# Moving the next block's norm behind attention, sending its scale through DRAM, and letting merge gates run up to six tiles ahead

## The chip, the cores and the metric

The kernel runs on one core of a Trainium2 chip. The metric is the device time of one execution in microseconds (us), as the median of several runs. Engines: PE (TensorE, matmuls), DVE (VectorE), ACT (ScalarE), POOL (GpSimd) and SP (SyncE, which here issues every DMA). Each engine works through its own instructions in order.

## The reference, cut to what matters

One layer of a hybrid decoder trunk over x of 2048 tokens by 1024 channels, in float32:

```python
h = _rmsnorm(x, norm_w[l])                    # x * rsqrt(mean(x*x) + EPS) * w
proj = h @ w_in[l]                            # three mixers' inputs and the merge gates' logits
y_a = _hgrn2_branch(...)                      # gated linear recurrence
y_b = _gated_deltanet_branch(...)             # chunked delta rule
y_c = _swa_sink_branch(...)                   # sliding-window attention
lifted = jnp.einsum('bsnc,ncd->bsnd', ys, w_branch[l])
gates = jax.nn.sigmoid(gate_logits.reshape(Bn, S, N_BRANCHES, D_MODEL))
merged = jnp.sum(gates * lifted, axis=2)
x = x + merged @ w_out[l]
...
return _rmsnorm(x, final_norm)
```

## The kernel before, in words

The 2048 tokens go through in four blocks of 512, block 0 to block 3 (`block(s, ...)`, called at the end of `_trunk`). Most operands are kept channel-major: a tile is 128 channels by 512 tokens. Every float32 product is done as three matmuls on a high and a low part (lines 101 to 103 in `mm_ct`, lines 169 to 171 in `mm_tc`), so one projection of 1024 channels onto 128 outputs is 24 matmuls of 512 columns (two weight tiles `wHL` of 12 matmuls each), and one lift of a branch's 512 channels is 12 (one weight tile). `load_w` (line 77) loads the weight tiles; there are four slots (`WB`). Block 0 loads raw weights, splits them on ACT and DVE and stores the split pair; blocks 1 to 3 load the stored pair (`wHL<-kept`, 512 KB).

A block runs, in the order in which it is written: four units of branch A, four of branch B (`unit_b`), four of branch C (`unit_c`, attention), with `merge(0)`, `merge(1)` and `merge(2)` after each branch. `merge(n, yT)` goes over eight tiles of 128 output channels. Per tile: a gate projection, which reads only the block's h (`hH`, `hL`); a tanh on ACT into `gth` (line 352; two slots); the lift of the branch's output y (lines 101 to 103 again, on `yH`, `yL`), whose 12 matmuls go by head, three for each of the four units of the branch; the product of both on DVE (line 358, and 361 from `merge(1)` on); and the sum into `msum` on POOL (line 362). A `gth` slot is free again when POOL has summed it. The gates and lifts use the PSUM tag `d`, which has four banks.

The next block's norm stands between `c0`, `c1` and `unit_c(2)`: eight tiles of x are loaded (`load_x`, line 126, two slots `xs`), ACT squares them and sums along the row (line 128), POOL adds the two halves and takes the power -1/2 (lines 132, 115, 116), POOL forms four diagonal tiles (line 137), PE multiplies them by ones (line 138), and ACT copies the result to R (line 140), which holds each token's scale in every partition. After `merge(2)`, `norm_h` multiplies the transposed x tiles by R on DVE (line 153; three `xT` slots), and splits them into `hH` and `hL` on ACT and DVE (lines 106, 107); those two are single-buffered. `output()` then multiplies the merged tiles by the output weights. Block 3 has no next block and so no norm at that place.

The order on each engine is not the written one. A list scheduler takes, on each engine, the first instruction in written order that its own model of the durations calls ready, subject to the slot counts, and that order is then fixed: an engine that waits at run time for one instruction doesn't take a later one. `tc.issue_after(i)` puts what is written inside it behind instruction i on i's engine.

Of the kernel before, what the change touches and what calls it, by code (L numbers as in the profile page):

```python
# [11 lines left out]
F32 = mybir.dt.float32  # L12
# [4 lines left out]
ALU = mybir.AluOpType  # L17
# [3 lines left out]
P = 128  # L21
D = 1024
KT = D // P
TB = 512
NT = TB // P
BW = 512
EPS = 1e-6
# [4 lines left out]
WB = 4  # L32
NTC = 324
SBK = 65
BSTEP = 16 * SBK
SLOT = ("w0", "w1", "w2", "w3", "w4", "w5", "w7", "raw")

# [14 lines left out]
def _trunk(tc, S, a, out):  # L52
    nc = tc.nc
# [4 lines left out]
    sb = _Aligned(ctx.enter_context(tc.tile_pool(name="sb", bufs=2)))  # L58
    ps = ctx.enter_context(tc.tile_pool(name="ps", bufs=4, space=PSUM))
    dram = ctx.enter_context(tc.tile_pool(name="dram", bufs=1, space=DRAM))  # L60

    V, A, G, T = nc.vector, nc.scalar, nc.gpsimd, nc.tensor
# [9 lines left out]
    def bank(tag="d", w=None):  # L72
        return ps.tile([P, 512], F32, name="ps_" + tag, tag=tag, bufs=4 if tag == "d" else 2)
# [16 lines left out]
                nc.sync.dma_start(kept[key], w[:, :, :n].bitcast(F32))  # L90
        return w[:, 0, :n], w[:, 1, :n]

    last_mm, last_act, last_ld = [None], [None], [None]

    def mm_ct(p, src, rh, rl, nk):
        for q in range(nk // 4):
# [8 lines left out]
    def split(dst_h, dst_l, src, scale):  # L105
        A.activation(dst_h, src, AF.Copy, scale=scale)
        V.scalar_tensor_tensor(dst_l, src, scale, dst_h.bitcast(F32), op0=ALU.mult, op1=ALU.subtract)
# [5 lines left out]
    def rsq(dst, src, mul, add, exp=mhalf4):  # L113
        n = src.shape[-1]
        G.tensor_scalar(dst, src, mul, add, op0=ALU.mult, op1=ALU.add)
        G.tensor_tensor(dst, dst, exp[:, :n], op=ALU.pow)
# [6 lines left out]
    def load_x(s, sq, i, tag="xs"):  # L123
        j, half = i // 2, i % 2
        t = sb.tile([P, TB], F32, name="xs", tag=tag, bufs=2)
        nc.sync.dma_start(t, a["x"][s * TB + j * P:s * TB + (j + 1) * P, half * TB:(half + 1) * TB])
        scrp = sb.tile([P, TB], BF16, name="scrp", tag="scrp", bufs=1)
        A.activation(scrp, t, AF.Square, accum_out=sq[:, j, half:half + 1])

    def norm_scale(sq):  # L130
        rs = sb.tile([P, NT], F32, name="rsx", tag="rsx")
        G.tensor_tensor(rs, sq[:, :, 0], sq[:, :, 1], op=ALU.add)
        rsq(rs, rs, 1.0 / D, EPS)
        rp = bank("c0")
        for j in range(NT):
            dg = sb.tile([P, P], F32, name="dg", tag="vn")
            G.tensor_tensor(dg, ident, rs[:, j:j + 1].broadcast_to([P, P]), op=ALU.mult)
            T.matmul(rp[:, j * P:(j + 1) * P], onesP, dg, start=True, stop=True)
        R = sb.tile([P, TB], F32, name="R", tag="R", bufs=1)
        A.copy(R, rp)  # L140
        return rs, R

    def load_xT(s, kt, tag="xT", bufs=3):
        t = sb.tile([P, TB], F32, name="xT", tag=tag, bufs=bufs)
        nc.sync.dma_start(t, a["xT"][kt, :, s * TB:(s + 1) * TB])
        return t

    def norm_h(R, xT, eng=(V, V)):
        hH = sb.tile([P, KT, TB], F32R, name="hH", tag="hH", bufs=1)
        hL = sb.tile([P, KT, TB], F32R, name="hL", tag="hL", bufs=1)  # L150
        for kt in range(KT):
            t = xT(kt)
            eng[kt % 2].tensor_tensor(t, t, R, op=ALU.mult)
            split(hH[:, kt, :], hL[:, kt, :], t, normw[:, kt:kt + 1])
        return [hH[:, kt, :] for kt in range(KT)], [hL[:, kt, :] for kt in range(KT)]
# [69 lines left out]
    gscr = dram.tile([NH, TB], F32, name="gscr", tag="gscr")  # L225
    zb = sb.tile([P, NT * SBK], F32, name="zb", tag="w2")
    G.memset(zb, 0.0)
    scrN = [dram.tile([2 * NT * NT, BSTEP], F32, name="scrN%d" % k, tag="scrN%d" % k) for k in range(2)]
    scrX = [dram.tile([2 * NT * NT, BSTEP], F32, name="scrX%d" % k, tag="scrX%d" % k) for k in range(2)]
    for t in scrX:  # L230
        flat = bass.AP(tensor=t.tensor, offset=t.offset, ap=[[NT * SBK, P], [1, NT * SBK]])
        nc.sync.dma_start(flat, zb[:, 0:NT * SBK])
    convw = cload("convw", a["convw"])
# [80 lines left out]
    def block(s, hH, hL, last=None):  # L314
# [32 lines left out]
        def merge(n, yT):  # L347
            yH, yL = [[t[:, k, :] for k in range(4)] for t in yT]
            for dt in range(KT):
                gp = proj_ct(37 + n * KT + dt)  # L350
                th = sb.tile([P, TB], F32, name="gth", tag="gth", bufs=2)
                A.activation(th, gp, AF.Tanh, scale=0.5)  # L352
                lp = bank()
                mm_ct(lp, a["wb"][n, dt], yH, yL, 4)
                if n == 0:
                    m = sb.tile([P, TB], F32, name="msum", tag="msum", bufs=KT + 1)
                    msum.append(m)
                    V.scalar_tensor_tensor(m, th, 1.0, lp, op0=ALU.add, op1=ALU.mult)
                else:
                    m = msum[dt]  # L360
                    V.scalar_tensor_tensor(th, th, 1.0, lp, op0=ALU.add, op1=ALU.mult)  # L361
                    G.tensor_tensor(m, m, th, op=ALU.add)  # L362
                if n == 2:
                    mH.append(sb.tile([P, TB], F32R, name="mH", tag=SLOT[dt]))
                    mL.append(sb.tile([P, TB], F32R, name="mL", tag="msum", bufs=KT + 1))
                    split(mH[dt], mL[dt], m, 0.5)
# [122 lines left out]
        def unit_b(h):  # L489
# [53 lines left out]
            for c2 in range(2):  # L543
# [4 lines left out]
                for ci in range(2):  # L548
# [12 lines left out]
            sN, sX = scrN[h % 2], scrX[h % 2]  # L561
            half = lambda t, r: bass.AP(tensor=t.tensor, offset=t.offset + (r // 64) * NT * 4 * BSTEP,
                                        ap=[[64, 64], [4 * BSTEP, NT], [1, 64]])
            diag = lambda t: bass.AP(tensor=t.tensor, offset=t.offset, ap=[[BSTEP, 32], [64, 16], [1, 16]])
            for r in (0, 64):
# [172 lines left out]
        def output():  # L738
            rt = [[None, None] for _ in range(NT)]
            sq = sb.tile([P, NT, 2], F32, name="sq", tag="sq")  # L740
            for half in range(2):
                fs = slice(half * 512, half * 512 + 512)
                for j in range(NT):
                    t = sb.tile([P, 512], F32, name="rt", tag=SLOT[half * 4 + j])
                    nc.sync.dma_start(t, a["x"][t0 + j * P:t0 + (j + 1) * P, fs])
                    rt[j][half] = t
                pj = mm_tc(a["wo"][half], 512, mH, mL, 4 if half and s == NSB - 1 else 1)
                for j in range(NT):
                    t = rt[j][half]
                    V.tensor_tensor(t, pj[j], t, op=ALU.add)  # L750
                    scrp = sb.tile([P, TB], BF16, name="scrp2", tag="scrp", bufs=1)
                    A.activation(scrp, t, AF.Square, accum_out=sq[:, j, half:half + 1])
                    if half == 0:
                        G.tensor_tensor(t, t, fnorm[:, fs], op=ALU.mult)
                    elif s == NSB - 1 and j < NT - 1:
                        V.tensor_tensor(t, t, fnorm[:, fs], op=ALU.mult)

            def final():
                for j in range(NT):
                    ss = sb.tile([P, 1], F32, name="ss2", tag="ss2", bufs=4)  # L760
                    G.tensor_tensor(ss, sq[:, j, 0:1], sq[:, j, 1:2], op=ALU.add)
                    rsq(ss, ss, 1.0 / D, EPS)
                    for half in range(2):
                        fs = slice(half * 512, half * 512 + 512)
                        t = rt[j][half]
                        if half == 0 or (s == NSB - 1 and j < NT - 1):
                            A.activation(t, t, AF.Copy, scale=ss)
                        else:
                            V.scalar_tensor_tensor(t, t, ss, fnorm[:, fs], op0=ALU.mult, op1=ALU.mult)
                        nc.sync.dma_start(out[t0 + j * P:t0 + (j + 1) * P, fs], t)  # L770
            return final
# [32 lines left out]
        f3(yB)  # L804
        c1 = unit_c(1)
        merge(1, yB)
        yC = new_y()
        c0(yC)
        c1(yC)
        if s + 1 < NSB:  # L810
            sq = sb.tile([P, NT, 2], F32, name="sqx", tag="sqx")
            with tc.issue_after(last_ld[0]):
                for i in range(2 * NT):
                    load_x(s + 1, sq, i)
            R = norm_scale(sq)[1]
        unit_c(2)(yC)
        unit_c(3)(yC)
        merge(2, yC)
        if s + 1 < NSB:
            return norm_h(R, lambda kt: load_xT(s + 1, kt)) + (output(),)  # L820
        output()()

    for s in range(NSB):
# [90 lines left out]
```

## Time and profile before

| | us |
|---|---|
| median of 3 runs | 2516.06 (2513.42 to 2519.41) |
| the profiled execution, device time | 2514.51 |
| its span, first to last instruction | 2512.7 |
| PE busy in the span | 2428.6 (97%) |
| DVE, ACT, POOL busy | 1170.9, 869.2, 434.2 |
| mean granted TensorE clock | 0.984 of full speed |

The span is the time between the first and the last instruction of the profiled execution; 1.8 us of the device time lie around it. A busy PE in these views is a PE with a matmul in flight: consecutive matmuls overlap and their ends are modelled, so that short waits between them hide in the busy time.

### The profile page before, as it was taken

The numbers are of one execution on the slowest core, as the hardware profiler recorded it, in microseconds if no ns is written. First come the engines' busy times: TensorE is split into PE (matmuls) and PEld (weight loads), VectorE is DVE, ScalarE is ACT, GpSimd is POOL, SyncE is SP. The second block draws the span as 40 slices with busy tenths as digits, with TensorE's granted clock in tenths as the row PEclk, the third lists the DMA queues.
The fourth block names the chain that finished last, engine by engine and source line by source line (L and its number), as shares of the span: only waits on it lengthen the run. The fifth ranks groups of instructions, "written<-read, shape, count | busy, mean of one in ns | idle before, by whom it ended". The sixth has DMA issues, their size and how long they took to land. (4 is left out here: it accounts for less than half of the span.)

```text
span 2512.7 us, 37478 instructions
## 1 busy us (share of the span) xinstructions
PE 2428.6 (97%) x13658; PEld 1946.4 (77%) x13658; DVE 1170.9 (47%) x3188; ACT 869.2 (35%) x2288; POOL 434.2 (17%) x821
## 2 busy tenths in 40 slices
PE   8999998999999999899999999989999999998998
PEld 7777776778877777678887877767888787876886
DVE  5666575465345535524214553551322455455321
ACT  5454344444334313323223422332322342233221
POOL 3221011211222101111112210111111221111111
PEclk9999998999999999999999999999999999999999
DMA  7756673769944455264774455425566354442555
GB/s 244 247 193 224 221 260 96 241 221 336 299 134 130 154 161 158 83 208 148 247 218 127 139 156 165 146 88 193 167 228 210 122 155 149 160 150 87 176 193 175
DMA packets 193156, 452.84 MB, mean 180 GB/s; under 512 B 52243, under 2 KB 70588, under 8 KB 192844
## 3 DMA queue, kind: packets, MB, share of 16 engines
q1 hardware_dynamic: 192972, 450.45, 55.3%
q8 instruction: 108, 1.77, 0.3%
q14 instruction: 76, 0.62, 0.1%
HBM read 348.81 MB, written 103.14 MB: 180 GB/s over the span
## 5 line engine op out<-in xcount | busy, mean ns | idle before, releaser
L101 PE MATMUL ps_d<-hH,wHL 128*128 128x512 f32 x1952 | 785.6, 402 | 4.1 <-DVE mm L700 2.2
L102 PE MATMUL ps_d<-hL,wHL 128*128 128x512 f32 x1952 | 783.5, 401 | 0.0
L103 PE MATMUL ps_d<-hH,wHL 128*128 128x512 f32 x1952 | 779.9, 400 | 0.7 <-DVE wHL L87 0.7
L101 PEld LDWEIGHTS ps_d<-hH,wHL 128*128 128x128 f32 x1952 | 369.4, 189 | 77.5 <-DVE mm L700 3.9
L103 PEld LDWEIGHTS ps_d<-hH,wHL 128*128 128x128 f32 x1952 | 369.3, 189 | 71.8 <-issue 1.8
L102 PEld LDWEIGHTS ps_d<-hL,wHL 128*128 128x128 f32 x1952 | 369.4, 189 | 68.0 <-issue 1.7
L87 DVE TENSOR_TENSOR wHL<-wraw,wHL 128x512 fp32r<-128x512 f32 (+1 forms) x194 | 130.6, 677 | 93.3 <-ACT wHL L86 91.2
L362 POOL TENSOR_TENSOR msum<-msum,gth 128x512 f32<-128x512 f32 x64 | 88.6, 1387 | 443.6 <-DVE gth L361 443.6
L101 PE MATMUL ps_d<-yH,wHL 128*128 128x512 f32 x384 | 155.3, 406 | 5.8 <-ACT yH L342 3.7
L86 ACT CAST wHL<-wraw 128x512 fp32r<-128x512 f32 (+1 forms) x194 | 113.7, 590 | 130.9 <-PE ps_d L103 80.8
L103 PE MATMUL ps_d<-yH,wHL 128*128 128x512 f32 x384 | 154.9, 403 | 0.0
L102 PE MATMUL ps_d<-yL,wHL 128*128 128x512 f32 x384 | 153.8, 401 | 0.1
L352 ACT ACTIVATE gth<-ps_d 128x512 f32<-128x512 f32 x96 | 57.3, 597 | 256.9 <-PE ps_d L103 256.1
L361 DVE SCALAR_TENSOR_TENSOR gth<-gth,ps_d 128x512 f32<-128x512 f32 x64 | 43.9, 687 | 184.9 <-PE ps_d L103 177.4
L169 PE MATMUL ps_d<-wHL,mH 128*128 128x512 f32 x256 | 99.7, 391 | 1.3 <-DMA wHL<-kept 1.3
L502 DVE SCALAR_TENSOR_TENSOR qkB<-raw,convw,qkB 128x512 f32<-128x512 f32 x96 | 71.7, 746 | 61.2 <-ACT qkB L500 59.9
L170 PE MATMUL ps_d<-wHL,mH 128*128 128x512 f32 x256 | 99.6, 389 | 0.0
L171 PE MATMUL ps_d<-wHL,mL 128*128 128x512 f32 x256 | 99.5, 389 | 0.0
L101 PEld LDWEIGHTS ps_d<-yH,wHL 128*128 128x128 f32 x384 | 73.0, 191 | 21.8 <-ACT yH L342 4.6
L102 PEld LDWEIGHTS ps_d<-yL,wHL 128*128 128x128 f32 x384 | 73.6, 192 | 15.9 <-DVE yL L343 1.7
L103 PEld LDWEIGHTS ps_d<-yH,wHL 128*128 128x128 f32 x384 | 73.5, 191 | 15.2 <-issue 0.5
L402 PEld LDWEIGHTS ps_c<-qk 128*64 128x64 f32 x1536 | 52.6, 137 | 33.3 <-issue 20.4
(281 smaller groups left out, 3761.0 us busy)
## 6 DMA issues: line engine op xcount, KB each, us to landing
wHL<-kept SPq DMA_DIRECT2D x486, 512.0 KB, 3.6
kept<-wHL SPq DMA_DIRECT2D x162, 512.0 KB, 4.0
wraw<-in_wct_dram SPq DMA_DIRECT2D x122, 256.0 KB, 3.7
wHL<-kept SPq DMA_DIRECT2D x32, 324.0 KB, 4.1
xT<-in_xT_dram SPq DMA_DIRECT2D x32, 256.0 KB, 4.6
xs<-in_x_dram SPq DMA_DIRECT2D x32, 256.0 KB, 4.4
rt<-in_x_dram SPq DMA_DIRECT2D x32, 256.0 KB, 4.6
out_dram<-rt SPq DMA_DIRECT2D x32, 256.0 KB, 4.0
```

The costliest lines, as they stand in the source:

```text
L86: A.copy(w[:, 0, :n], raw[:, :n])
L87: V.tensor_tensor(w[:, 1, :n], raw[:, :n], w[:, 0, :n].bitcast(F32), op=ALU.subtract)
L101: T.matmul(p, wh[:, ks], rh[kt], start=(kt == 0), stop=False)
L102: T.matmul(p, wh[:, ks], rl[kt], start=False, stop=False)
L103: last_mm[0] = T.matmul(p, wl[:, ks], rh[kt], start=False, stop=(kt == nk - 1)).ins
L169: T.matmul(pj[j][:, :n], lh[kt][:, js], wh, start=(kt == 0), stop=False)
L170: T.matmul(pj[j][:, :n], lh[kt][:, js], wl, start=False, stop=False)
L171: T.matmul(pj[j][:, :n], ll[kt][:, js], wh, start=False, stop=(kt == KT - 1))
L352: A.activation(th, gp, AF.Tanh, scale=0.5)
L362: G.tensor_tensor(m, m, th, op=ALU.add)
L402: T.matmul(sp[g * 64:g * 64 + 64, c * 32:(c + 1) * 32], K[:, c * P + g * 64:c * P + g * 64 + 64], qv[:, c, g * nb // 2:(g + 1) * nb // 2, ...
L502: V.scalar_tensor_tensor(dst, raw[:, j:j + TB], convw[:, ti, j:j + 1], dst, op0=ALU.mult, op1=ALU.add)
```

## The change

`norm_scale` is no longer called between blocks (only at the start of the kernel). The loads of x, the squares and POOL's sum and power now stand behind `unit_c(2)` and `unit_c(3)` and in front of `merge(2)`. In place of POOL's diagonal tiles, the matmuls by ones and the copy on ACT, SP writes the 512 scales to a row in DRAM (4 from each of 128 partitions) and reads that row back into all 128 partitions. `norm_h`'s DVE instructions are put behind the last line-361 instruction of `merge(2)`. The slots of `gth` go from two to six, in all three merges.

```diff
+GB = 6
...
+    rscr = dram.tile([TB], F32, name="rscr", tag="rscr")
+
+    def norm_row(sq):
+        rs = sb.tile([P, NT], F32, name="rsx", tag="rsx")
+        G.tensor_tensor(rs, sq[:, :, 0], sq[:, :, 1], op=ALU.add)
+        rsq(rs, rs, 1.0 / D, EPS)
+        nc.sync.dma_start(rscr.rearrange("(j p) -> p j", p=P), rs)
+        R = sb.tile([P, TB], F32, name="R", tag="R", bufs=1)
+        nc.sync.dma_start(R, rscr.rearrange("(o t) -> o t", o=1).broadcast_to([P, TB]))
+        return R
...
-                th = sb.tile([P, TB], F32, name="gth", tag="gth", bufs=2)
+                th = sb.tile([P, TB], F32, name="gth", tag="gth", bufs=GB)
...
-                    V.scalar_tensor_tensor(th, th, 1.0, lp, op0=ALU.add, op1=ALU.mult)
+                    last_dve[0] = V.scalar_tensor_tensor(th, th, 1.0, lp, op0=ALU.add, op1=ALU.mult).ins
...
         c1(yC)
+        unit_c(2)(yC)
+        unit_c(3)(yC)
         if s + 1 < NSB:
             sq = sb.tile([P, NT, 2], F32, name="sqx", tag="sqx")
             with tc.issue_after(last_ld[0]):
                 for i in range(2 * NT):
                     load_x(s + 1, sq, i)
-            R = norm_scale(sq)[1]
-        unit_c(2)(yC)
-        unit_c(3)(yC)
+            R = norm_row(sq)
         merge(2, yC)
         if s + 1 < NSB:
-            return norm_h(R, lambda kt: load_xT(s + 1, kt)) + (output(),)
+            with tc.issue_after(last_dve[0]):
+                hs = norm_h(R, lambda kt: load_xT(s + 1, kt))
+            return hs + (output(),)
         output()()
```

## Rows read from the trace of the kernel before

**Rows 1.** The page: span, busy times of the engines, granted clock in 40 slices.
```profile
span 2512.7 us, 37478 instructions
PE 2428.6 (97%) x13658; PEld 1946.4 (77%) x13658; DVE 1170.9 (47%) x3188; ACT 869.2 (35%) x2288; POOL 434.2 (17%) x821
...
PEclk9999998999999999999999999999999999999999
```

**Rows 2.** Busy time by window, merge 1's last line 361 to merge 2's first; blocks 0-3.
```profile
core 0: us, PE busy (x) PEld busy (x) DVE busy (x) ACT busy (x) POOL busy (x), PEclk, DMA share, GB/s
499.90:552.90 53.00, 50.94 (x279) 40.21 (x278) 32.63 (x95) 26.25 (x71) 6.25 (x12) 0.97 0.64 224
1117.30:1173.00 55.70, 51.05 (x292) 40.94 (x291) 24.94 (x82) 23.72 (x66) 5.80 (x13) 0.97 0.42 141
1736.50:1793.60 57.10, 51.66 (x292) 41.34 (x291) 24.98 (x83) 23.13 (x64) 5.78 (x13) 0.94 0.41 135
2356.30:2404.70 48.40, 48.37 (x283) 38.80 (x282) 24.07 (x79) 19.80 (x55) 1.68 (x1) 1.00 0.40 131
```

**Rows 3.** Waits of PE (who for whom: total us, times, longest us).
```profile
PE ps_c L138 <- POOL dg L137: 14.3, 5, 5.4
```

**Rows 4.** The norm of block 1 in order of time (start, us; in brackets idle before).
```profile
1124.65 0.63 ACT L128 ACTIVATE scrp<-xs 128x512 bf16<-128x512 f32 x1 [1.70 <-DMA xs<-in_x_dram]
...
1128.33 0.20 POOL L132 TENSOR_TENSOR rsx<-sqx 128x4 f32<-128x4 f32 x1 [8.98 <-ACT scrp L128]
...
1130.44 1.22 PE L138 MATMUL ps_c<-dg,onesP 128*128 128x128 f32 x4 [4.64 <-POOL dg L137]
...
1133.03 0.59 ACT L140 COPY R<-ps_c 128x512 f32<-128x512 f32 x1 [4.79 <-PE ps_c L138]
```

**Rows 5.** Busy time by window: the stretch ahead of merge 1, blocks 0 and 1.
```profile
368.00:449.00 81.00, 67.54 (x360) 51.43 (x359) 48.06 (x165) 33.51 (x105) 10.60 (x22) 0.87 0.32 102
989.00:1066.40 77.40, 69.50 (x396) 52.40 (x395) 43.16 (x154) 28.86 (x95) 9.80 (x22) 0.95 0.28 86
```

**Rows 6.** Busy time by window: the last 8.1 us of that stretch, blocks 0-3.
```profile
440.40:448.50 8.10, 5.36 (x23) 4.17 (x24) 5.08 (x17) 2.34 (x8) 1.75 (x4) 0.74 0.31 98
1058.30:1066.40 8.10, 4.94 (x25) 3.43 (x24) 4.98 (x17) 2.62 (x8) 1.29 (x3) 0.94 0.21 65
1677.70:1685.80 8.10, 4.94 (x28) 3.41 (x27) 5.08 (x17) 2.40 (x9) 1.47 (x4) 1.00 0.20 65
2297.30:2305.40 8.10, 4.94 (x25) 3.39 (x24) 4.97 (x17) 2.63 (x8) 1.30 (x4) 0.94 0.22 68
```

**Rows 7.** Block 1 at that place in order of time: PE, then ACT's third gate.
```profile
1058.22 0.40 PE L103 MATMUL ps_d<-hH,wHL 128*128 128x512 f32 x1
...
1062.70 0.33 PE L338 MATMUL ps_c<-ident,LT 128*128 128x128 f32 x1 [1.60 <-ACT LT L336]
...
1064.52 0.73 PE L101 MATMUL ps_d<-yH,wHL 128*128 128x512 f32 x2 [1.02 <-ACT yH L342]
...
1068.48 0.60 ACT L352 ACTIVATE gth<-ps_d 128x512 f32<-128x512 f32 x1 [0.34 <-POOL msum L362]
```

**Rows 8.** Busy time by window: merge 2 of block 1, the output behind it.
```profile
1173.00:1226.00 53.00, 53.00 (x235) 43.91 (x234) 11.98 (x18) 10.44 (x17) 8.99 (x7) 1.00 0.72 236
1226.00:1268.00 42.00, 42.00 (x186) 34.63 (x185) 11.98 (x18) 7.58 (x16) 6.94 (x7) 1.00 0.76 234
```

**Rows 9.** Line 128 (squares), ACT's idle time before them, in blocks 0, 1, 2 each.
```profile
  DMA xs<-in_x_dram: 8.8, 6
...
  DMA xs<-in_x_dram: 12.1, 7
...
  DMA xs<-in_x_dram: 12.9, 7
```

**Rows 10.** Line 126 in block 1: SP's waits before the x loads (ns min/median/max).
```profile
L126 SPq EVENT_SEMAPHORE  x6: 17/22/2482, 1110.6 to 1120.6; - x6
```

**Rows 11.** DMA issues: KB each, median us from issue to landing.
```profile
wHL<-kept SPq DMA_DIRECT2D x486, 512.0 KB, 3.6
xs<-in_x_dram SPq DMA_DIRECT2D x32, 256.0 KB, 4.4
LT<-gscr SPq DMA_DIRECT2D x16, 256.0 KB, 3.5
L<-scrN SPq DMA_DIRECT2D x16, 32.0 KB, 3.0
```

**Rows 12.** Groups by line: the three instructions per tile of `norm_h`.
```profile
L106 ACT ACTIVATE hH<-xT,normw 128x512 fp32r<-128x512 f32 x32 | 22.0, 719 | 21.8 <-DVE xT L153 21.5 <-POOL xT L153 0.3
L153 DVE TENSOR_TENSOR xT<-xT,R 128x512 f32<-128x512 f32 x28 | 20.2, 747 | 28.3 <-ACT R L140 18.5 <-DMA xT<-in_xT_dram 9.7
```

**Rows 13.** Block 1 in order of time: last half of h, ACT.
```profile
1238.38 0.72 ACT L106 ACTIVATE hH<-xT,normw 128x512 fp32r<-128x512 f32 x1 [1.71 <-DVE xT L153]
```

More of the change, by code (lines that the diff above doesn't have):

```diff
@@ L91, in load_w @@
         return w[:, 0, :n], w[:, 1, :n]
-    last_mm, last_act, last_ld = [None], [None], [None]
+    last_mm, last_act, last_ld, last_dve = [None], [None], [None], [None]
     def mm_ct(p, src, rh, rl, nk):
```

## The prediction, on record before the result was known

> **What bounds the kernel now.** I read the page's busy times first: PE has a matmul in flight for 2428.6 of 2512.7 us, the other engines are far behind [rows 1]. So only two things can move the time: less PE work, or fewer places where PE stands. The second has to be looked for by stage, because the shares are averages; the table of windows shows it. Three kinds of window matter here.
>
> In merge 2 and in the output PE is busy for the whole 53.0 and 42.0 us at full clock [rows 8]; nothing can be won there except by removing matmuls. 235 matmuls in 53.0 us are 0.2255 us each, so a gate projection (24) is 5.4 us and a lift (12) is 2.7 us.
>
> Between merge 1's last product and merge 2's first, blocks 0, 1 and 2 take 53.0, 55.7 and 57.1 us, block 3 takes 48.4 [rows 2]. The same four attention units' work is in all four; only block 3 has no norm for a successor. In block 3 PE is busy for 48.37 of 48.40 us, in block 1 for 51.05 of 55.70, with a clock of 0.97. The waits of PE name the place: line 138, the matmul by ones, waits for POOL's diagonal tiles, 14.3 us in five waits [rows 3]. In order of time in block 1 [rows 4]: ACT waits 1.70 us for a tile of x, POOL starts 8.98 us after it could, PE then stands 4.64 us.
>
> Ahead of merge 1 (units 2 and 3 of branch B with the first attention units) PE is busy 67.54 of 81.0 us in block 0 and 69.50 of 77.4 in block 1 [rows 5]; blocks 2 and 3 repeat block 1 to 0.1 us. Here PE waits for a chain of short steps, and has too little independent work to put between them.
>
> **The change part by part.** *The norm leaves PE's path.* Removed from PE, per block: eight passes of line 138 and the wait for them. I don't add up instructions; block 3 already runs this stretch without them. The difference is 53.0 - 48.4 = 4.6, 55.7 - 48.4 = 7.3, 57.1 - 48.4 = 8.7 us, together **-20.6 us** [rows 2]. It includes what the lower clock behind the wait costs (0.97 and 0.94 against 1.00 in the same rows: part of the stretch is at 1.2 instead of 2.4 GHz). Block 0 also splits weights there, so block 3 is a rough measure for it; its own idle PE, 53.0 - 50.94 = 2.1 us, plus the eight passes is near enough to 4.6.
>
> *Its replacement.* Loads, squares and POOL's work are the same, now while unit 3 of branch C ends and merge 2 begins. POOL's power to the landing of R: the row's write I bound by L<-scrN, 3.0 us, the broadcast by LT<-gscr, the same shape, 3.5 us [rows 11]. Both are on nobody's path: R is needed after merge 2's last product, and merge 2 alone lasts 53 us [rows 8]. If merge 2 did not cover them they would cost 6.5 us a block.
>
> The cost that remains is the waiting engines. ACT now waits for x among the exponentials and copies of the last attention unit. In the old place these waits were 8.8, 12.1 and 12.9 us [rows 9]; ACT is busy for about 24 of 48 us there (19.80 to 26.25) [rows 2], so most falls into idle time. What PE sees is how much later ACT runs than the fixed order supposed. From below: zero. From above: 4.64 us, PE's own wait at the end of that same chain [rows 4], three times, 13.9 us. I take 2 us a block, **+6 us**, below the middle because gates can stand between. SP holds the weight loads behind its waits: for a slot of x it stood up to 2.48 us [rows 10]. Four weight tiles are 4 x 2.7 = 10.8 us of matmuls, a load lands in 3.6 us [rows 11], so up to 7.2 us of standing SP is covered. I take zero, and 6.5 us a block as the upper end.
>
> A rule that speaks against this edit: the Trainium skill (DMA: Bandwidth & Descriptors, Specifications) states that pieces under 512 B make the DMA engine read, modify and write, and the new row is written in 4-byte pieces. No row here has 4-byte pieces; by that rule the write would take longer than its bound above, and, as merge 2 has room for several times that, the sum would stay.
>
> *norm_h.* Its multiplies now all follow merge 2; before, three of eight ran early. That is 3 x 0.75 = 2.2 us more of DVE [rows 12] in front of h. The last half of h was ready at 1239.1 in block 1 [rows 13] and is first read after the output, which runs to beyond 1268 [rows 8]: 29 us of cover. Zero; it would cost 2.2 us a block otherwise.
>
> *Six gate slots.* Where they bite is seen in block 1 [rows 7]: PE ended the third gate's projection at 1058.22, but its tanh came at 1068.48, released by POOL's sum, that is by a `gth` slot. In between PE waits 1.60 us for one chain step and 1.02 us for the next. In that stretch of 8.1 us PE is idle for 8.1 - 5.36 = 2.7 us in block 0 and 8.1 - 4.94 = 3.2 us in each other block [rows 6]. With a free slot the tanh runs at once, its PSUM bank comes free, and the third lift's nine matmuls (2.0 us) and half of the fourth gate (2.7 us) can go there. So **-2.7 - 3 x 3.2 = -12.3 us**. It is not all of the 13.5 and 7.9 us idle ahead of merge 1 [rows 5], because lifts that wait for the last head hold their PSUM bank and weight tile: of four each, two are taken before 1058. The bounds are zero (these hold as firmly as the slots did) and 13.5 + 3 x 7.9 = 37.2 us. In merges 0 and 2 I count nothing; block 3 has no idle PE ahead of merge 2 [rows 2].
>
> *Sum.* 2514.5 (the profiled execution; the median is 1.5 us more) - 20.6 - 12.3 + 6 = 2487.6, said as **2488 us**, 1.1% faster.
>
> **The rivals.**
> 1. *Gates fill everything.* With six slots the whole idle time ahead of merge 1 goes: 2514.5 - 20.6 - 37.2 + 6 = 2463. For it: the idle time is there in four blocks. Against it: four PSUM banks and four weight tiles.
> 2. *Gates change nothing*, since banks or tiles bind first: 2514.5 - 20.6 + 6 = 2500. The one that would show the change not doing what it says; the tanh released by POOL [rows 7] speaks against it.
> 3. *The wait moves.* ACT's waits for x now delay the last attention unit by 4.64 us a block, and PE, in fixed order, stands at the lift's last head; with the gates as forecast 2514.5 - 20.6 - 12.3 + 13.9 = 2496, with no gain from gates 2508.
> 4. *Slower: weight tiles run out.* Freed from `gth`, the scheduler opens lifts up to the number of banks. Each keeps its weight tile until the branch's last unit is done. Once four are open, no gate's weights can be loaded; when y arrives PE finishes four lifts' last heads (12 matmuls, 2.7 us) and then waits for a load of 3.6 us [rows 11]. That is felt in front of each of 12 merges, 43 us: 2514.5 - 20.6 + 43 = 2537. It decides from the fourth lift opened ahead. Against it: at 1058 two are open and eight microseconds are left.
>
> The Trainium skill (DMA: Bandwidth & Descriptors, Anatomy of one DMA) says that a DMA's semaphore wait happens on the issuing sequencer before dispatch; SP's 2.48 us in front of a load of x [rows 10] agree. By it the new row's two DMAs would hold the loads behind them, which is the zero to 6.5 us a block above; fully uncovered that is 19.5 us and about 2507.
>
> **How the numbers follow.** Forecast (2476 to 2500) 0.50; rival 1 0.15; rival 2 0.12; rival 3 or an uncovered SP (2496 to 2513) 0.12; rival 4 0.11. The range leaves out rival 4 and the far ends of 1 and 3: 2460 to 2509. A measurement of this kernel tells about 0.2% (5 us) from no change. Faster by more: 0.82. Within 0.2%: 0.07, from the far end of rival 3 and a weak rival 4. Slower: 0.11.
>
> **What would show it.** Right: no line 138 after the start; the stretch of rows 2 near 48 to 51 us in every block with PE busy throughout; the third tanh of merge 1 within a microsecond of its projection; PE's idle time ahead of merge 1 down by about 3 us a block; `norm_h` ending before the output. Wrong: a PE wait at the lift's last head in front of merge 2 as long as the old wait at line 138 (rival 3); PE waiting for wHL<-kept at the start of merges (rival 4); SP standing several microseconds at the row's DMAs. What makes the whole number fall is a scheduler that, given other slots, orders the B chain otherwise than before.

## The result, and the profile after

The changed kernel takes 2506.47 us (median of 7 runs, 2502.98 to 2512.8), the kernel before in the same series 2519.41 us (median of 7, 2513.42 to 2534.69). The ratio is 0.9944, 95% interval 0.9926 to 0.9963: 0.56% faster, where 1.1% was forecast. The profiled execution takes 2505.49 us, against 2514.51.

Line numbers: `load_w`'s lines are one further than before (L83, L86 to L88), from `norm_scale` on everything is 12 further; the new lines are L137 (the row's write) and L139 (R's read).

From the page: the span, the busy times, the clock in 40 slices [rows 1].

```profile
span 2503.6 us, 37412 instructions
...
PE 2418.3 (97%) x13634; PEld 1935.1 (77%) x13634; DVE 1178.4 (47%) x3188; ACT 865.7 (35%) x2285; POOL 431.1 (17%) x809
...
PEclk9999998999999999999999999999999999999999
```

Again PE is busy for 97%; its busy time is 10.3 us less and the span 9.1 us. Where they went is in the windows. Busy time between merge 1's last product (line 373) and merge 2's first, blocks 0 to 3, columns as in [rows 2]:

```profile
499.40:551.20 51.80, 49.74 (x278) 39.21 (x277) 31.59 (x93) 31.80 (x86) 4.22 (x8) 1.00 0.86 244
1114.80:1168.20 53.40, 50.21 (x285) 40.51 (x284) 23.95 (x79) 25.11 (x72) 4.91 (x9) 0.97 0.68 163
1730.00:1785.80 55.80, 51.08 (x286) 41.24 (x285) 23.99 (x80) 25.26 (x72) 4.92 (x9) 0.94 0.65 156
2347.40:2395.80 48.40, 48.38 (x284) 38.77 (x283) 24.01 (x80) 19.79 (x55) 1.68 (x1) 1.00 0.40 131
```

53.0, 55.7 and 57.1 us have become 51.8, 53.4 and 55.8, not 48.4. The clock in blocks 1 and 2 is what it was, and PE is still idle for 3 to 5 us. What PE waits for there has another name [rows 3]; waits of PE before, then of PE and of SP in the changed kernel, each over the whole kernel (who for whom: total us, times, longest):

```profile
PE ps_c L723 <- DVE E L716: 3.7, 6, 0.8
```

```profile
PE ps_c L735 <- DVE E L728: 11.8, 14, 1.6
...
PE ps_d L102 <- DMA wHL<-kept: 8.3, 3, 4.2
```

```profile
SPq L139 <- DMA rscr<-rsx: 23.3, 3, 10.0
```

Of the three waits for stored weights (`wHL<-kept`), two lie in the norm stretch, 2.73 us in block 1 and 4.24 us in block 2. The third, 1.29 us, stands at the start of block 1, where the kernel before waits 1.63 us. SP stands three times, up to 10.0 us, at the issue of R's read, until the row has landed. SP in block 1 in order of time, how long a row's write takes to land, how long block 1's load behind it takes, and PE at the end of that:

```profile
1148.27 0.38 SPq L137 DMA_DIRECT2D rscr<-rsx  x1
1148.73 0.46 SPq L83 DMA_DIRECT2D wHL<-kept  x1
1159.24 0.32 SPq L139 DMA_DIRECT2D R<-rscr  x1
1159.61 0.90 SPq L83 DMA_DIRECT2D wHL<-kept  x2
```

```profile
DMA to landing us min/median/max: 8.9/8.9/8.9
```

```profile
DMA to landing us min/median/max: 11.9/11.9/11.9
```

```profile
1160.72 0.50 PE L102 MATMUL ps_d<-hH,wHL 128*128 128x512 f32 x1 [2.73 <-DMA wHL<-kept]
```

The write of 2 KB lands 8.9 us after its issue (the prediction bounded it at 3.0). That is block 2's, the only one of the three whose landing the profile tells; in block 1 SP's read goes out 10.97 us behind the write. The 512 KB load issued 0.46 us behind it lands after 11.9 us, where 3.6 is usual [rows 11]. Two things are thus late together: SP, and the load that did get out. The experiments have to part them.

A sum by stage, in us over four blocks, between the same products on DVE in each kernel. "Ahead of merge 1" runs here from merge 0's last product to merge 1's first, so it holds all of branch B; a merge runs from its first product to its last. "Lost" is a stretch's length less the usual spacing (the median for that shape of matmul) of all PE instructions in it, so it holds what half clock costs too.

| stage | before | changed | changed, again |
|---|---|---|---|
| ahead of merge 1: length / lost | 561.0 / 86.5 | 560.3 / 76.8 | 561.2 / 77.7 |
| merge 1: length / lost | 203.8 / 3.0 | 198.1 / 6.9 | 197.7 / 6.5 |
| norm stretch, blocks 0-3 | 53.0, 55.7, 57.1, 48.4 | 51.8, 53.5, 55.7, 48.4 | 51.6, 53.8, 55.8, 48.4 |
| merge 2: length | 209.7 | 206.1 | 206.1 |
| all else: length | 1324.0 | 1329.7 | 1331.2 |

Merge 2 is shorter in part because two to five of its lift matmuls a block now stand ahead of its first product; it belongs with the norm stretch. The last column is a second profiled execution on another chip (the last experiment): each stage but the last row agrees to 0.9 us, the last to 1.5. Single executions of one kernel differ by some 15 us all the same, since stretches at half granted clock come and go elsewhere; so the experiments are read by stage, and their medians beside that. One such stretch, in block 1 of the eighth experiment just ahead of merge 0's first product, and the same place in the changed kernel:

```profile
840.80:861.30 20.50, 20.50 (x76) 13.04 (x75) 6.63 (x22) 4.76 (x11) 0.52 (x1) 0.50 0.16 49
```

```profile
843.00:863.50 20.50, 20.50 (x127) 15.37 (x128) 11.01 (x31) 8.23 (x23) 3.08 (x8) 1.00 0.33 103
```

PE is busy throughout in both, with 76 matmuls in the one and 127 in the other, at a granted clock of 0.50 and 1.00 (1.2 and 2.4 GHz). The code of that place is the same in both. That is 10 us and more, the size of what is to be measured.

**The gates.** The last 8.1 us ahead of merge 1's first product, blocks 0 to 3 [rows 6], and in block 1 the last matmul of the third gate's projection and its tanh [rows 7]:

```profile
440.90:449.00 8.10, 6.32 (x32) 4.74 (x32) 5.27 (x19) 2.99 (x11) 1.48 (x4) 0.93 0.29 98
1057.40:1065.50 8.10, 6.98 (x35) 4.73 (x34) 5.17 (x17) 2.77 (x8) 1.38 (x4) 1.00 0.21 66
1672.70:1680.80 8.10, 6.99 (x35) 4.76 (x34) 5.17 (x17) 2.77 (x8) 1.36 (x4) 1.00 0.21 65
2290.10:2298.20 8.10, 6.98 (x35) 4.79 (x34) 5.08 (x18) 2.84 (x9) 1.31 (x4) 1.00 0.21 67
```

```profile
1057.42 0.40 PE L104 MATMUL ps_d<-hH,wHL 128*128 128x512 f32 x1
```

```profile
1058.71 0.58 ACT L364 ACTIVATE gth<-ps_d 128x512 f32<-128x512 f32 x1
```

The tanh comes 1.3 us after that matmul's start, where it was 10.3 us. PE's busy time rose by 0.96 us in block 0 and by 2.04 or 2.05 in each other, the third lift's nine matmuls; the half of the fourth gate that was to follow isn't there. Instead, PE and DVE just behind the lifts in block 1:

```profile
1068.30 0.39 PE L102 MATMUL ps_d<-hH,wHL 128*128 128x512 f32 x1
1070.28 0.44 PE L735 MATMUL ps_c<-ident,E 128*128 128x128 f32 x2 [1.60 <-DVE E L728]
```

```profile
1065.54 1.88 DVE L373 SCALAR_TENSOR_TENSOR gth<-gth,ps_d 128x512 f32<-128x512 f32 x3
1067.66 1.22 DVE L723 TENSOR_TENSOR es<-es,rsum 128x4 f32<-128x4 f32 x1 [0.24 <-ACT E L720]
1068.91 0.18 DVE L724 RECIPROCAL es<-es 128x4 f32<-128x4 f32 x1
1069.12 1.89 DVE L728 TENSOR_SCALAR E<-E,es 128x256 f32<-128x256 f32 x4
```

PE waits 1.60 us for attention's scaled exponentials E. The third lift, which stood behind the branch's end before and covered them, is already done. So part of the gain is given back where merge 1 starts.

`norm_h` stays hidden: its last half in block 1 starts at 1237.04 [rows 13], inside the output.

```profile
1237.04 0.73 ACT L107 ACTIVATE hH<-xT,normw 128x512 fp32r<-128x512 f32 x1 [0.16 <-DVE xT L165]
```

### The profile page after: what moved, and what is told of

Read it like the earlier page. It is cut to its first block, busy times and chain, and to the rows that moved or that the text cites. A ratio compares the mean times of both kernels' runs of the same rounds, so it can differ in the third digit from the quotient of the medians.

```text
span 2503.6 us, 37412 instructions
## 1 busy us (share of the span) xinstructions
PE 2418.3 (97%) x13634; PEld 1935.1 (77%) x13634; DVE 1178.4 (47%) x3188; ACT 865.7 (35%) x2285; POOL 431.1 (17%) x809
## 5 line engine op out<-in xcount | busy, mean ns | idle before, releaser
L88 DVE TENSOR_TENSOR wHL<-wraw,wHL 128x512 fp32r<-128x512 f32 (+1 forms) x194 | 131.3, 681 | 96.0 <-ACT wHL L87 92.2
```

Of the source, the lines that this page charges most:

```text
L88: V.tensor_tensor(w[:, 1, :n], raw[:, :n], w[:, 0, :n].bitcast(F32), op=ALU.subtract)
```

## The experiments

The theory that these rows suggest: the gates give about half of what was forecast, and the norm's gain is lost to the row's 4-byte pieces, through SP, which stands for them. The first four experiments ran on one chip, the next four on a second, the last two on a third, each series with its own runs of the kernel before. Of the versions meant to be faster than the changed kernel, only the last can be told from it by its median; the intervals of the others overlap with the changed kernel's, and what they show is read by stage, from one profiled execution each.

**Each half alone.** The kernel before with six gate slots:

```diff
+GB = 6
...
-                th = sb.tile([P, TB], F32, name="gth", tag="gth", bufs=2)
+                th = sb.tile([P, TB], F32, name="gth", tag="gth", bufs=GB)
```

> The kernel before with six gate slots and nothing else; the norm stays in its old place. The two parts add: then about 6 us less than before (ratio 0.9975, 0.9965 to 0.9985), which is what the stretches ahead of merge 1 and merge 1 itself gained in the changed kernel, with the third gate's tanh within 1 us of its projection and the fourth gate still behind the branch's end. Rival, the gates serve as cover for the norm's waits only: no gain without the norm's move (ratio 1.000).

Measured: 2516.49 us, ratio 0.9988 [0.9972, 1.0004]. Ahead of merge 1 lost 79.2 (86.5 before), in merge 1 6.7 (3.0): together 3.6 us better. Norm stretch and merge 2 together 421.8 instead of 424.0. The new wait for E stands here too: 1.6 us where merge 1 starts, in every block.

The changed kernel with two slots:

```diff
-GB = 6
+GB = 2
```

> The changed kernel with two gate slots, that is the norm's move alone. The parts add: 6 to 8 us less than before (ratio 0.997, 0.996 to 0.9985), and PE's waits for weight tiles in front of merge 2 as in the changed kernel (three, 8 us). Rival, the move needs the gates as cover: no gain or a loss (ratio 1.000 or more) with longer waits at the lift's last head.

Measured: 2516.77 us, ratio 0.9986 [0.9967, 1.0006]. Norm stretch 209.2 and merge 2 205.8, together 415.0: the norm alone is worth 9.0 us. The wait for E where merge 1 starts is gone. Neither half alone can be told from no change in the median. By stage the norm gives alone what it gives with the gates (9.0 and 8.5 us), the gates somewhat less (3.6 and 5.8).

**Is it SP that stands?** R's read goes behind the weight loads of merge 2's fifth tile, so that SP waits for nothing:

```diff
             for dt in range(KT):
...
+                if dt == at:
+                    R = norm_read()      # R's read, behind last_ld[0]
...
-        merge(2, yC)
+        R = merge(2, yC, 4 if s + 1 < NSB else None)
```

> The changed kernel with one DMA moved: the read of the row into all partitions is issued behind the weight loads of merge 2's fifth tile, so that SP doesn't stand for the row's write with weight loads behind it. Theory SP (SP standing for the write, 23.3 us in three waits, is what starves PE): PE's waits for stored weight tiles go from 8.3 us to under 2, each of blocks 0 to 2 gets 2 to 4 us shorter, 6 to 12 us in all (ratio to before 0.990 to 0.992). Theory ACT (the squares' waits for x delay the attention units): the time stays within 2 us of the changed kernel (ratio 0.994), PE still stands in the same place, now for the exponentials.

Measured: 2511.53 us, ratio 0.9967 [0.9951, 0.9983]; norm stretch 54.8, 54.1, 53.3, 48.4. SP no longer stands, and PE waits as before: SP in block 1, the landings of these loads, and PE.

```profile
1150.93 0.38 SPq L137 DMA_DIRECT2D rscr<-rsx  x1
1151.40 9.49 SPq L83 DMA_DIRECT2D wHL<-kept  x3
```

```profile
DMA to landing us min/median/max: 5.9/12.3/12.8
```

```profile
1163.71 0.80 PE L102 MATMUL ps_d<-hH,wHL 128*128 128x512 f32 x1 [3.16 <-DMA wHL<-kept]
```

The theory in this form falls. Theory ACT doesn't hold either, since PE's waits for weights stay (7.5 us instead of 8.3). Two loads are issued 0.5 and 1.5 us behind the row's write, and land after 12.3 and 12.8 us: the pieces hold the loads themselves.

**Are the pieces the cause?** The row is written in 128 pieces of 16 bytes, in another order, which the multiply then reads back in steps (1.08 instead of 0.69 us each in the median, hidden):

```diff
-        nc.sync.dma_start(rscr.rearrange("(j p) -> p j", p=P), rs)
+        nc.sync.dma_start(rscr.rearrange("(p j) -> p j", p=P), rs)
```

> The changed kernel with the row written in 128 pieces of 16 bytes instead of 512 of 4; the row's tokens then stand in another order, and the multiply reads R with a stride of 16 bytes. If the write's time goes with its pieces, SP stands about 3 us for it instead of 10 and most of the gain of the late read comes here too (ratio 0.990 to 0.993). If it is a fixed cost of so small a write, SP stands 8 us or more and the time is that of the changed kernel. The strided multiplies may take longer than 0.69 us; they are beside the output's matmuls, so nothing by itself.

Measured: 2503.22 us, ratio 0.9939 [0.9917, 0.9961]. Landing of the row's write, and the windows of the norm stretch:

```profile
DMA to landing us min/median/max: 2.7/2.9/3.1
```

```profile
500.20:551.80 51.60, 49.72 (x278) 39.19 (x277) 31.59 (x92) 31.84 (x86) 4.27 (x8) 1.00 0.72 245
1116.20:1165.60 49.40, 48.68 (x286) 39.27 (x285) 23.96 (x80) 25.19 (x72) 4.85 (x9) 1.00 0.56 176
1735.10:1785.00 49.90, 48.62 (x286) 39.22 (x285) 23.90 (x80) 25.17 (x72) 4.88 (x9) 1.00 0.56 174
2346.60:2395.00 48.40, 48.39 (x284) 38.76 (x283) 24.02 (x80) 19.77 (x55) 1.68 (x1) 1.00 0.41 131
```

The write lands in 2.7 and 3.1 us (two of the three are told), and the load behind it in block 1 in 4.4 instead of 11.9. The stretch is 10.0 us shorter than in the changed kernel, nearly all of it in blocks 1 and 2, at full clock. This is the cause of the missing norm gain. The median shows little of the 10 us (ratio 0.9939 against 0.9944), and by it the two can't be told apart. This profiled execution has 20.1 us at half clock in the output and branch A, 7.7 in the changed kernel's; why the other executions gain as little isn't shown.

**The same write from another queue**, with the late read, parts "in the same queue" from "on the same DMA engines":

```diff
-        nc.sync.dma_start(rscr.rearrange("(j p) -> p j", p=P), rs)
+        nc.scalar.dma_start(rscr.rearrange("(j p) -> p j", p=P), rs)
```

> The kernel with the late read, whose row of 512 4-byte pieces is now issued by ACT on a DMA queue of its own instead of SP's. With the late read alone SP was free, yet the two weight loads issued behind the row's write landed 12.3 and 12.8 us after their issue (3.6 is usual) and PE still waited 7.5 us for them. Theory A (pieces hold what stands behind them in the same queue): on another queue the loads pass, land in under 6 us, PE's wait at line 102 for wHL goes, the norm stretch falls from 210.6 to 199 to 202 us over four blocks. Theory B (the pieces occupy the DMA engines themselves, whatever the queue): landings of 8 us and more stay, PE's wait stays at 5 to 8 us, the stretch at 207 to 211.

Measured: 2499.44 us, ratio 0.9935 [0.9913, 0.9957]; norm stretch 56.1, 49.9, 49.6, 48.4. Neither expectation holds whole. The load issued 1.3 us behind the write in block 2 still lands late:

```profile
DMA to landing us min/median/max: 11.7/11.7/11.7
```

In block 1 it is 9.2 us. So the pieces hold loads of another queue too (theory B); the Trainium skill (DMA: Bandwidth & Descriptors, Issuing engines are not separate DMA queues) says that DMAs of all issuing engines run on the same 16 DMA engines, and these landings agree. But of PE's 7.5 us of waits at line 102, 6.4 stood behind the row, and these are gone (the 1.9 us left are at the start of block 1). That was A's forecast, for another reason: a write issued by ACT does not stand between SP's loads in SP's fixed order, and the load that PE needs next went out 0.7 us (block 1) and 1.4 us (block 2) ahead of it. What counts is which load stands behind the pieces. Block 0's 56.1 holds 3.4 us at half clock; the rest of it was not traced.

**Do weight tiles bound the gates?** Six instead of four in the changed kernel, then with the 16-byte pieces too:

```diff
-        w = sb.tile([P, 2, 512], F32R, name="wHL", tag="wHL", bufs=WB)
+        w = sb.tile([P, 2, 512], F32R, name="wHL", tag="wHL", bufs=6)
```

> The changed kernel with six weight tiles instead of four; all else is the same. Theory (weight tiles bound the gates): in the changed kernel the fourth gate of merge 1 had to wait for a lift to give its tile back. With two more tiles it runs before the branch ends, the 1.98 us in which PE waits at 1068.3 us goes, and PE's lost time ahead of merge 1 falls from 76.8 us by about 2 us a block to some 68. Six tiles hold 16.2 us of matmuls, so the weight loads held back at the norm's row should be mostly covered as well: PE's wait of 8.3 us for wHL at line 102 falls to 0 to 4 and the stretch between merge 1 and merge 2 (209.4 us over four blocks) to 200 to 205. Together 10 to 17 us less than the changed kernel, about 2490 to 2497 us. Rival (PSUM banks or the B chain itself bound the gates): PE's lost time ahead of merge 1 stays within 2 us of 76.8; then only the norm stretch changes, 4 to 9 us.

> Six weight tiles, and the row written in 128 pieces of 16 bytes. If tiles bounded the gates and pieces held the weight loads, the two gains stand in different stages and add up: norm stretch as with the 16-byte pieces alone (199.4 us over four blocks, less 1 at most), lost PE ahead of merge 1 about 68 instead of 77. In all 8 to 12 us less than with the 16-byte pieces alone: about 2492 us. Rival (both remove the same standing of SP): no faster than the better of the two alone, 2497 to 2503.

Measured: 2500.8 us, ratio 0.9941 [0.992, 0.9962], and 2497.11 us, 0.9928 [0.9906, 0.9949]. Lost ahead of merge 1 is 80.8 and 82.8 us, not 68. The same wait stands at the same place of block 1:

```profile
1067.41 0.44 PE L735 MATMUL ps_c<-ident,E 128*128 128x128 f32 x2 [1.57 <-DVE E L728]
```

The theory falls: the order ahead of merge 1 is what it was with four tiles. The time came from elsewhere. In the first, PE's waits for weights at line 102 are gone and the norm stretch is 205.3, though PE's waits for E rose from 11.8 to 18.6 us; in both, output and branch A take 801.0 and 802.4 us instead of 807.5 (803.8 before). In the second the stretch is 208.2, with 10.2 us at half clock in block 0 (58.4; blocks 1 and 2: 50.6, 50.8).

**ACT's waits for x.** With 16-byte pieces, loads and squares return to the old place, ahead of units 2 and 3; only the row stays ahead of merge 2:

```diff
-        unit_c(2)(yC)
-        unit_c(3)(yC)
         if s + 1 < NSB:
...
                     load_x(s + 1, sq, i)
+        unit_c(2)(yC)
+        unit_c(3)(yC)
+        if s + 1 < NSB:
             R = norm_row(sq)
```

> 16-byte pieces, with the loads of x and their squares back in the old place, in front of attention units 2 and 3; the row stays in front of merge 2. Theory (ACT's waits for x among the last unit's exponentials delay PE): PE's wait for the scaled exponentials E in front of their transposes falls from 13.4 us to 4 to 6, and the norm stretch from 199.4 to 195 to 197 us over four blocks (block 3, without a norm, is 48.4, four times that 193.6). Rival (what is left is not ACT's): the stretch stays at 198 to 200; if the squares disturb unit 2 instead, 200 to 203.

Measured: 2500.64 us, ratio 0.9935 [0.991, 0.996]. The windows of the norm stretch, and PE's wait for E (13.4 us in 12 with the squares late):

```profile
500.40:547.40 47.00, 46.95 (x268) 37.59 (x267) 31.10 (x94) 26.21 (x69) 2.75 (x6) 1.00 0.71 248
1126.20:1174.60 48.40, 48.40 (x284) 38.95 (x283) 23.11 (x80) 22.56 (x63) 4.23 (x9) 1.00 0.50 163
1740.60:1789.10 48.50, 48.50 (x284) 38.84 (x283) 23.15 (x79) 23.27 (x65) 4.23 (x9) 1.00 0.52 169
```

```profile
PE ps_c L739 <- DVE E L732: 9.8, 9, 1.7
```

Blocks 1 and 2 are now as short as block 3, with PE busy throughout; 1.0 and 1.4 us of the 49.4 and 49.9 had been ACT's. Of the 13.4 us of waits for E, 3.6 stood in the norm stretches, and none of these is left. (Block 0's stretch holds ten matmuls fewer than with the late squares, so its 47.0 is not all gain.) It is this profiled execution that ran 27.3 us at half clock in block 1, ahead of merge 0's first product.

**All three mends**, beside the changed kernel on the same chip:

> 16-byte pieces, squares in the old place, and six weight tiles. Theory (the three act in different places): norm stretch 192 to 195 us over four blocks, as with the early squares and four tiles (192.2); outside it the 6 to 10 us that six tiles gave at the weight loads of the output, branch A and branch B; no gain ahead of merge 1, where six tiles left the order as it was (80.8 and 82.8 us of lost PE, 76.8 with four). About 2490 us, against 2497.1 with six tiles and 16-byte pieces alone. Rival (with six tiles the scheduler takes work away from PE's waits for the scaled exponentials, which rose from 13.4 to 18.9 us): the stretch stays at 200 us or more, about 2497.

> The changed kernel itself, on the same chip as the version with all three mends, so that the two can be set side by side: 2503 to 2508 us, norm stretch 208 to 211 us over four blocks.

Measured: 2486.02 us (2481.54 to 2491.93), ratio 0.9862 [0.9827, 0.9897], and 2507.56 us, 0.9954 [0.9932, 0.9977]. The intervals are apart: the mended version is 21.5 us faster than the change as made. Its norm stretch:

```profile
496.90:546.30 49.40, 49.18 (x278) 39.42 (x277) 31.43 (x92) 26.59 (x70) 2.79 (x5) 1.00 0.70 244
1111.40:1159.70 48.30, 48.30 (x283) 38.80 (x282) 23.05 (x79) 21.21 (x59) 4.23 (x9) 1.00 0.44 151
1721.70:1769.40 47.70, 47.70 (x281) 38.33 (x280) 23.07 (x79) 21.21 (x59) 4.23 (x9) 1.00 0.44 149
```

Stretch and merge 2 together 401.1 us (424.0 before, 415.5 in the change as made), output and branch A 801.5, and ahead of merge 1 no gain (lost 76.3), as expected.

## Why the prediction was right and wrong

The sign, the bound and the range (2460 to 2509) hold; the size does not. The sum was -20.6 + 6 - 12.3 = -26.9 us, the span lost 9.1. The difference comes in three parts of about 6 us each: the norm, the gates, and what the sum left out elsewhere. By stage:

- **The norm off PE's path, -20.6 + 6 = -14.6; measured -8.5** (424.0 to 415.5, stretch and merge 2). The step that failed is the row's price: L<-scrN, 3.0 us, was taken for the write, and what it does to the weight loads, SP's standing among it, was put at zero. The row that the price was taken from is a read of 32 KB, not a write in 4-byte pieces. The write took 8.9 us and more, and made the loads behind it late by about as much. With this one thing mended the stretch is 14.9 us shorter than before, with merge 2 18.5: block 3 was a fair measure of what can be won, and this term of the sum would have held. The upper end for an uncovered SP, 19.5 us, contained the 10.0 measured, but named half of the mechanism: freeing SP alone didn't bring it back.
- **The rule on pieces under 512 B** (the Trainium skill, DMA: Bandwidth & Descriptors, Specifications) had the direction: the write was slower than its bound. What was drawn from it, "the sum would stay", was wrong. Merge 2 covers R, but not the loads that share the DMA engines with the row. The rule alone does not part 8.9 from 2.7 and 3.1 us, as 4 and 16 bytes are both under 512; the runs changed size and number of pieces together (512 to 128), so which counts is open.
- **ACT's waits for x, +6.** What 16-byte pieces leave above 48.4 in blocks 0 to 2 is 3.2 + 1.0 + 1.5 = 5.7 us. Moving the squares back brought blocks 1 and 2 to 48.4 and 48.5. Block 0's part can't be told from its different work. Rival 3's size for this, 13.9 us, did not come.
- **Six gate slots, -12.3; measured -5.8** (lost ahead of merge 1 -9.7, in merge 1 +3.9; by length -6.4). The step that failed is the half of the fourth gate, and the assumption that nothing else would make PE stand. The first half of the step is right to the row: the tanh comes with its projection, nine matmuls of the third lift follow, 2.0 us a block. The second half, the fourth gate, did not come. Rival 4's tiles are not why: with six the order is the same. Whether the four PSUM banks or the scheduler's own durations keep it back was not tried. And a stall came that the sum had left out, the 1.6 us in which PE waits for E in blocks 1 to 3. Every version with six slots has it; the kernel before has 0.8 us in one block, and two slots with the norm moved have none. In these rows E is late on DVE, where the sum of line 723 takes 1.22 us, with 0.163 as its median, and the first scaling behind it 1.10, with 0.348 as its median: together 1.8 us, more than PE's wait (the last section has what runs beside them).
- **Elsewhere +5.7** (1324.0 to 1329.7, 1331.2 in the second execution), which the sum didn't have. Of it, 3.7 us are in output and branch A; there six tiles take it back; by what path four tiles lose it was not traced.
- Right as put: no line 138 between blocks, `norm_h` inside the output, no gain for PE in merge 2. Rivals 1, 2 and 4 did not happen. The number given for an SP whose standing is fully uncovered, about 2507, was met within two microseconds by luck, from other terms. One reading was loose: block 2's stretch ahead of merge 1 is 0.4 us longer than block 1's, not equal to 0.1 us; its idle PE is the same 7.9 us.

## What to carry to other kernels

A transfer in tiny pieces can have two prices: its own landing, and the delay of the loads behind it on the same DMA engines. Cost a row in tiny pieces by a row of the trace with pieces like it, and if there is none, put its upper end on the loads that the busy engine needs next, not on the reader of the row. When a stall is filled with work brought forward, look for the stall that this work used to cover, and for the engines on which its other steps now run together; and where executions differ by as much as the effect, compare stages between fixed instructions.

## What the runs showed of the hardware

2 KB from 128 partitions to a row in DRAM landed, where the profiles tell it, in 8.9 to 10.0 us as 512 pieces of 4 bytes, and in 1.4 to 5.0 us as 128 pieces of 16 bytes. In blocks where the landing isn't told and SP waits for it, SP's read went out 10.4 to 11.5 us behind a 4-byte row. A 512 KB load issued within 2 us behind the 4-byte row landed in 9.2 to 13.5 us, whichever engine had issued the row.

The DMA packets in the traces show where this time is spent. In block 1 of the changed kernel 528 packets of 4 bytes start 0.90 to 1.27 us behind the write's issue and take 7 to 9 ns each. The 4 KB packets of the load that start 1.7 to 2.2 us behind the issue are the ones that stand, 16 of them for 2.5 to 8.9 us, where the median is 0.16. Data packets of over 3 us number 59 in the changed kernel (48 to 65 in the other versions with 4-byte pieces and four weight tiles, 6 with six tiles), none in the kernel before, and none in any version with 16-byte pieces. So the pieces are soon out of the way, and the loads' first packets behind them wait; for what, the traces don't tell.

DVE's sum over 128x4 elements (line 723) took 1.22 us in the rows above. All its executions in the changed kernel (ns min/median/max), and POOL's sums of line 374 beside the one above:

```profile
L723 DVE TENSOR_TENSOR es<-es,rsum x32: 154/163/1247, 398.0 to 2389.3; 128x4 f32<-128x4 f32 x32
```

```profile
1066.31 3.77 POOL L374 TENSOR_TENSOR msum<-msum,gth 128x512 f32<-128x512 f32 x3 [4.88 <-DVE gth L373]
```

The three sums end at 1067.61, 1068.86 and 1070.08; the DVE instruction ends at 1068.88, just behind the second. Four of the 32 took 1.2 us, one in each block, and the others 0.15 to 0.29. In all twelve traces those of 1.2 us end 0.02 us behind one of these sums of POOL. So it looks as if DVE had waited for POOL's instruction to end, but no run moved POOL's sums away, and it is not tested.
